# The end of a one-core transformer layer: last bank's weights gated ahead of their split, second rows' last bank in halves, squares on VectorE, epsilon as a column

## The chip, the cores and the metric

The kernel runs on one core of a Trainium2 chip. The metric is device time in microseconds (us), the median over several executions. A core has five engines, each with its own instruction queue that it works through in order: TensorE (PE; PEld is its loading of stationary weights), VectorE (DVE), ScalarE (ACT), GpSimd (POOL) and SyncE (SP, which here only issues DMAs). They wait for each other by semaphores. SBUF is the on-chip memory of 128 partitions, PSUM the banks into which TensorE adds up its products.

## The reference

One layer over 256 latent tokens of width 2048 (and 256 context tokens): a half-step feed-forward network (FFN), token mixing, a second half-step FFN, then a final RMSNorm. What the change touches is the end of the second FFN and the norm behind it. In the reference's words:

```python
def rms_norm(x, g):
    xf = x.astype(jnp.float32)
    y = xf * lax.rsqrt(jnp.mean(xf * xf, axis=-1, keepdims=True) + RMS_EPS)
    return (y * g.astype(jnp.float32)).astype(x.dtype)

def half_step_ffn(x, mod, i, g, w_up, w_down):
    h = adaln(x, g, mod, i)
    a, b = jnp.split(h @ w_up, 2, axis=-1)
    return x + 0.5 * mod[:, i + 2, None, :] * ((jax.nn.silu(a) * b) @ w_down)
...
        xl = half_step_ffn(xl, mod_l, 6, g_norm[l, 2], w_ffn2_up[l], w_ffn2_down[l])
    return rms_norm(xl, g_final)
```

So per output column there is a gate (0.5 times a modulation row) and a gain (`g_final`), and per token one factor, the reciprocal root of the mean square plus epsilon, which needs all 2048 columns of that token.

## The kernel before

The products are made close to float32 accuracy out of pairs of reduced-precision values. `split` (L120 on) makes from a 128x2048 weight tile `raw` a rounded part `hi` (a copy by ScalarE, L128) and the rest `lo` (a subtraction by VectorE, L129), in two halves of 1024 columns. `mm3` (L152) then issues three matmuls per product: stationary hi with moving hi, stationary lo with moving hi, stationary hi with moving lo. In the last part the stationary operand is 128 tokens of the hidden activations, and the moving one is up to 512 columns of weights.

The 5632 hidden units of the second FFN are taken in groups of 512. The down projection of a group has four weight tiles of 1 MB, one for each bank `cb` of 512 output columns (`CB`); each tile holds four blocks of 128 hidden units (`FB`). `down` works through two groups at a time and adds the results into `acc2`, an SBUF tile of the 256 tokens: `t = 0` is the first 128 of them (the first rows), `t = 1` the second. After the group before the last, `down` also multiplies `acc2` by the gate (`half_gated`, L1030) and has GpSimd start a DMA that adds the residual `x2d` into it (`accum`, L731).

The last group is done by `last2`. It loads its four weight tiles through SP; tiles 0 and 1 go whole into buffers of their own (`hi0`, `lo0` and so on), tiles 2 and 3 through `load_split`. Then, for t = 0 and t = 1 and within each for the four banks: `block` issues 12 matmuls into a PSUM bank, VectorE gates the result (`half_gated` into `sab`) and adds it to `acc2` (L2323), ScalarE squares the sum and adds up along the row (`sumsq`, L163), and VectorE multiplies by the gain in place (`gain`, L2291), one block later than the square that reads the same columns. `ended` closes a half of the tokens: VectorE sums the four partial sums (L2296), multiplies by 1/D and adds epsilon (L2298), GpSimd raises to the power -1/2 (L2299), then ScalarE scales banks 0 and 1 (L2308) and VectorE banks 2 and 3 (L2306; for the second rows' bank 3 gain and factor in one operation, L2304), and SP stores each bank (L2309). The first rows' `ended` is a generator whose two parts are stepped between the second rows' blocks.

The order on each engine is the program's order where an instruction is pinned (`pin`), and otherwise what a scheduler made of it; within one engine nothing overtakes. In-place work on `acc2` makes waits: the gain may only overwrite a bank when its square has been read.

Of the kernel before, what the change touches and what calls it, by code (L numbers as in the profile page):

```python
# [19 lines left out]
P = 128  # L20
# [38 lines left out]
def tile_layer(ctx: ExitStack, tc: tile.TileContext, I: dict, out: bass.AP):  # L59
# [13 lines left out]
    def bank():  # L73
        return ps["mm"].tile([P, 512], F32, tag="mm", name="mm")
# [45 lines left out]
    def split(raw, n=2048):  # L120

        half = n // 2
        parts = []
        for h in range(2):
            hi = wp.tile([P, 1024], F32R, tag="hi", name="hi", bufs=4)[:, :half]
            lo = wp.tile([P, 1024], F32R, tag="lo", name="lo", bufs=4)[:, :half]
            src = raw[:, h * half : (h + 1) * half]
            scalar[0].activation(hi, src, AF.Copy)  # L128
            vector[0].tensor_tensor(lo, src, hi.bitcast(F32), op=ALU.subtract)  # L129
            parts.append((hi, lo))  # L130

        def at(w):
            h, o = divmod(w.start, half)
            return tuple(x[:, o : o + w.stop - w.start] for x in parts[h])

        return at
# [24 lines left out]
    def sumsq(dst, x, n=512):  # L161
        junk = sm.tile([P, 512], BF16, tag="junk", name="junk", bufs=1)
        scalar[0].activation(junk[:, :n], x, AF.Square, accum_out=dst)  # L163
# [103 lines left out]
    class Beside:  # L267
# [49 lines left out]
        def steps(self):  # L317
            half = None
            while self.n < len(self.items) or self.due or self.late:
                while self.n < len(self.items):  # L320
                    h = self.items[self.n][2]
                    if h != half:
                        half = h
                        conditions({LAT: self.cB}, h, h + 1, (LAT,))
                        self.waits += WAIT
                    if self.n not in self.slots or self.done < np.interp(self.n, *zip((0, 0), *self.pace)) + self.waits:
                        break
                    self.one()
                yield
                self.done += 1  # L330
                for x in [x for x in self.due if x[0] <= self.done]:
                    self.due.remove(x)
                    self.finish(*x[1:])
                if self.late and self.late[0][0] <= self.done:
                    mod_rows_out(*self.late.pop(0)[1:])

    def pin(ins):
        tc.keep_in_program_order(ins)
# [58 lines left out]
    def drain(it):  # L397
        for _ in it:
            pass
# [62 lines left out]
    with pool(name="st", bufs=1) as st:  # L462
# [53 lines left out]
        def factor(ss4):  # L516
            s1 = sm.tile([P, 1], F32, tag="s1", name="s1")
            vector[0].tensor_reduce(s1, ss4, axis=AX.X, op=ALU.add)
            r = sm.tile([P, 16], F32, tag="rstd", name="rstd", bufs=4)[:, :1]
            vector[0].tensor_scalar(r, s1, 1.0 / D, EPS, op0=ALU.mult, op1=ALU.add)  # L520
            nc.gpsimd.tensor_tensor(r, r, mhalf[:, :1], op=ALU.pow)
            return r
# [505 lines left out]
    def half_gated(a, y, g, sign=1.0):  # L1028

        nc.vector.scalar_tensor_tensor(a, y, 0.5 * sign, g, op0=ALU.mult, op1=ALU.mult)  # L1030
# [897 lines left out]
    with f2x:  # L1928
# [4 lines left out]
        def sab_tile():  # L1933
            return f2.tile([P, CB], F32, tag="sab", name="sab")
# [262 lines left out]
                                nc.scalar.activation(sab[t], bs[t], AF.Silu)  # L2197
                    yield

        def block(b, n, wt, t, first=True, last=True):  # L2200

            tt = slice(t * P, (t + 1) * P)
            for j in range(FB):
                w = slice(j * CB, (j + 1) * CB)
                mm3(b, hids[n][0][:, j, tt], hids[n][1][:, j, tt], *wt(w), first and j == 0, last and j == FB - 1)
            return b

# [67 lines left out]
        def last2():  # L2275

            parts = []
            for cb in range(NCB):
                if cb >= 2:
                    parts.append(load_split(I["w_dn2"][LAST, cb]))  # L2280
                    continue
                raw = raw_tile()
                nc.sync.dma_start(raw, I["w_dn2"][LAST, cb])
                hi = f3.tile([P, 2048], F32R, tag=f"f{2 * cb}", name=f"hi{cb}")
                lo = f3.tile([P, 2048], F32R, tag=f"f{2 * cb + 1}", name=f"lo{cb}")
                nc.scalar.activation(hi, raw, AF.Copy)
                nc.vector.tensor_tensor(lo, raw, hi.bitcast(F32), op=ALU.subtract)
                parts.append(lambda w, hi=hi, lo=lo: (hi[:, w], lo[:, w]))
            def gain(t, cb):
                a = acc2[:, t, cb * CB : (cb + 1) * CB]  # L2290
                pin(nc.vector.tensor_tensor(a, a, late["gf"][:, cb * CB : (cb + 1) * CB], op=ALU.mult))  # L2291

            def ended(t, ss):

                s1 = sm.tile([P, 1], F32, tag="s1", name="s1")
                pin(nc.vector.tensor_reduce(s1, ss, axis=AX.X, op=ALU.add))  # L2296
                r = sm.tile([P, 16], F32, tag="rstd", name="rstd", bufs=4)[:, :1]
                pin(nc.vector.tensor_scalar(r, s1, 1.0 / D, EPS, op0=ALU.mult, op1=ALU.add))  # L2298
                nc.gpsimd.tensor_tensor(r, r, mhalf[:, :1], op=ALU.pow)  # L2299
                for cb in (0, 2, 1, 3):  # L2300
                    c = slice(cb * CB, (cb + 1) * CB)
                    a = acc2[:, t, c]
                    if t and cb == 3:
                        pin(nc.vector.scalar_tensor_tensor(a, a, r, late["gf"][:, c], op0=ALU.mult, op1=ALU.mult))  # L2304
                    elif cb >= 2:
                        pin(nc.vector.tensor_scalar(a, a, r, None, op0=ALU.mult))  # L2306
                    else:
                        nc.scalar.activation(a, a, AF.Copy, scale=r)  # L2308
                    nc.sync.dma_start(out[t * P : (t + 1) * P, c], a)  # L2309
                    if not t and not cb:  # L2310
                        yield


            sss = [sm.tile([P, 4], F32, tag="ss4", name="ss4", bufs=4) for _ in range(2)]
            first = ended(0, sss[0])
            for t in range(2):
                for cb in range(NCB):
                    c = slice(cb * CB, (cb + 1) * CB)
                    b = block(bank(), LAST, parts[cb], t)
                    a = acc2[:, t, c]  # L2320
                    y = sab_tile()
                    half_gated(y, b, late["g8"][:, c])
                    nc.vector.tensor_tensor(a, a, y, op=ALU.add)  # L2323
                    sumsq(sss[t][:, cb : cb + 1], a)
                    if cb or t:
                        gain(*divmod(4 * t + cb - 1, 4))
                    if t:
                        steps(first)
            drain(ended(1, sss[1]))

        last2()

# [94 lines left out]
```

## Time and profile before

| | |
|---|---|
| median of 3 runs | 2600.66 us (2600.51 to 2602.32) |
| the profiled execution | 2601.07 us |
| its span, first to last instruction | 2599.4 us |
| PE busy | 2572.7 us (99%) |
| DVE busy | 2189.6 us (84%) |
| ACT busy | 1429.8 us (55%) |
| POOL busy | 220.9 us (8%) |
| last matmul starts | 2588.41 us |
| last weight tile issued | 2562.79 us |
| last power on POOL starts | 2592.58 us |

Rows of an engine in order of time read: start and length in us, engine, source line, operation, what it writes and reads, form, and in brackets the idle time before it with what ended it. An `xN` at the end means N such instructions merged, their length running from the first start to the last end. Instructions of one engine overlap a little in the records: the step from one start to the next is what one costs in a full queue. Window rows give, for a stretch, the busy time of each engine, the granted clock of TensorE (1.00 is full) and the DMA traffic.

### The profile page before, as it was taken

The page shows a single profiled execution, that of the slowest core. Times are in us where ns is not written, and L with a number is a line of the kernel's source. Part 1 is how long each engine was busy: PE and PEld are TensorE (multiplying, and loading weights), DVE is VectorE, ACT ScalarE, POOL GpSimd, SP SyncE. Part 2 cuts the span into 40 slices and gives each one's busy share as a digit, 9 for nine tenths or more (in the row PEclk, how much of TensorE's full clock was granted, in tenths as well). Part 3 has the DMA queues.
Part 4 walks back from the last instruction along what each step waited for, and adds up shares of the span by engine and source line. Part 5 has one row for each costly group of instructions (what it writes and reads, how often), then busy time and mean ns, then how long its engine had stood idle before and what let it go on. Part 6 is the DMA issues. An engine that isn't in the chain of part 4 may idle for free. (4 is left out here: it accounts for less than half of the span.)

```text
span 2599.4 us, 34147 instructions
## 1 busy us (share of the span) xinstructions
PE 2572.7 (99%) x12646; PEld 2139.5 (82%) x12646; DVE 2189.6 (84%) x2884; ACT 1429.8 (55%) x1838; POOL 220.9 (8%) x271
## 2 busy tenths in 40 slices
PE   8999999999999999999999999999999999999998
PEld 5788888888888878888889889888898788888886
DVE  7788888878888788888887888798889788898887
ACT  5454444554444555444454448456486676666663
POOL 0000000100000100000110000120000000000001
PEclk9999999999999999999999999999999999999999
DMA  9889999999999989889987886775768999999985
GB/s 397 349 216 266 270 284 273 260 275 285 260 286 270 275 238 243 217 217 223 227 258 263 295 318 241 238 278 214 265 237 245 266 272 278 288 285 278 271 250 168
DMA packets 127655, 684.71 MB, mean 263 GB/s; under 512 B 14200, under 2 KB 16760, under 8 KB 64896
## 3 DMA queue, kind: packets, MB, share of 16 engines
q1 hardware_dynamic: 98112, 490.63, 50.2%
q0 software_dynamic: 29376, 191.90, 37.5%
q8 instruction: 99, 1.62, 0.2%
q14 instruction: 68, 0.56, 0.1%
HBM read 664.59 MB, written 17.89 MB: 263 GB/s over the span
## 5 line engine op out<-in xcount | busy, mean ns | idle before, releaser
L128 ACT ACTIVATE hi<-raw 128x1024 fp32r<-128x1024 f32 (+2 forms) x488 | 505.4, 1040 | 412.4 <-PE mm L152 309.3
L129 DVE TENSOR_TENSOR lo<-raw,hi 128x1024 fp32r<-128x1024 f32 (+2 forms) x476 | 568.9, 1204 | 143.6 <-ACT hi L128 121.7
L128 ACT ACTIVATE hi<-chain 128x1024 fp32r<-128x1024 f32 x352 | 371.9, 1060 | 310.5 <-PE mm L152 169.5
L129 DVE TENSOR_TENSOR lo<-chain,hi 128x1024 fp32r<-128x1024 f32 x352 | 426.6, 1221 | 109.9 <-ACT hi L128 100.7
L152 PE MATMUL mm<-hi,hhi 128*128 128x512 f32 (+3 forms) x1024 | 394.0, 385 | 0.0
L152 PE MATMUL mm<-lo,hhi 128*128 128x512 f32 (+3 forms) x1024 | 387.0, 378 | 0.0
L152 PE MATMUL mm<-hi,hlo 128*128 128x512 f32 (+3 forms) x1024 | 386.4, 377 | 0.0
L208 DVE SCALAR_TENSOR_TENSOR junk<-sraw,cBh 128x1024 fp8e5<-128x1024 f32 x192 | 234.4, 1221 | 16.2 <-DMA sraw<-in_w_mt 14.0
L152 PEld LDWEIGHTS mm<-lo,hhi 128*128 128x128 f32 x1024 | 192.4, 188 | 34.2 <-DVE lo L129 0.3
L152 PEld LDWEIGHTS mm<-hi,hlo 128*128 128x128 f32 x1024 | 192.8, 188 | 30.7
L152 PEld LDWEIGHTS mm<-hi,hhi 128*128 128x128 f32 x1024 | 192.6, 188 | 31.0
L129 DVE TENSOR_TENSOR lo<-ra,hi 128x1024 fp32r<-128x1024 f32 x104 | 126.1, 1221 | 30.9 <-ACT hi L128 27.0
L128 ACT ACTIVATE hi<-ra 128x1024 fp32r<-128x1024 f32 x104 | 109.8, 1061 | 66.1 <-PE mm L152 35.2
L152 PE MATMUL mm<-hi,hid2h 128*128 128x512 f32 x352 | 137.1, 389 | 0.0
L152 PE MATMUL mm<-lo,hid2h 128*128 128x512 f32 x352 | 137.0, 389 | 0.0
L152 PE MATMUL mm<-hi,hid2l 128*128 128x512 f32 x352 | 137.0, 389 | 0.0
L152 PE MATMUL mm<-hi,sumshl 128*128 128x512 f32 x400 | 123.2, 389 | 0.0
L731 POOL DMA_DIRECT2D chain<-in_w_up1b x60 | 53.0, 884 | 727.7 <-DVE lo L129 727.7
L208 DVE SCALAR_TENSOR_TENSOR sr<-sr,cBl 128x1024 f32<-128x1024 f32 x84 | 102.0, 1222 | 13.4 <-DMA sr<-in_w_mt 6.4
L152 PE MATMUL mm<-hi,sumshh 128*128 128x512 f32 x352 | 108.4, 389 | 0.0
L152 PE MATMUL mm<-hhi,hi 128*128 128x512 f32 (+1 forms) x288 | 101.3, 352 | 0.0
L152 PE MATMUL mm<-hhi,lo 128*128 128x512 f32 (+1 forms) x288 | 99.0, 344 | 0.0
(490 smaller groups left out, 5453.8 us busy)
## 6 DMA issues: line engine op xcount, KB each, us to landing
raw<-in_w_dn SPq DMA_DIRECT2D x70, 1024.0 KB, 10.1
chain<-in_w_up1b POOLq DMA_DIRECT2D x60, 1024.0 KB, 10.2
sraw<-in_w_mt SPq DMA_DIRECT2D x96, 512.0 KB, 8.0
sr<-in_w_mt SPq DMA_DIRECT2D x81, 512.0 KB, 5.6
raw<-in_w_up1b SPq DMA_DIRECT2D x40, 1024.0 KB, 7.7
mraw<-in_w_m SPq DMA_DIRECT2D x32, 1024.0 KB, 7.5
chain<-in_w_dn POOLq DMA_DIRECT2D x30, 1024.0 KB, 8.4
chain<-in_w_up2b POOLq DMA_DIRECT2D x28, 1024.0 KB, 12.6
```

Source lines behind the costliest of these rows:

```text
L128: scalar[0].activation(hi, src, AF.Copy)
L129: vector[0].tensor_tensor(lo, src, hi.bitcast(F32), op=ALU.subtract)
L152: tensor[0].matmul(out_ap, s, m, start=first and not n, stop=last and n == 2, skip_group_check=skip)
L208: ins = nc.vector.scalar_tensor_tensor(junk() if junk else raw, raw, 1.0, cB[s], op0=ALU.mult, op1=ALU.mult, accum_out=mT[:, i, s, kt, h : ...
L731: accum = lambda dst, src: nc.gpsimd.dma_start(dst, src, accum_op=ALU.add)
```

## The change

All of it is in `last2`, apart from a column offset `c0` in `block`.

- The last weight tile (`cb == 3`) is multiplied by the gate in place, four times 128x512 by VectorE, before `split`. The block of that bank then needs no gating: VectorE adds PSUM straight into `acc2`.
- The gain row `gf` is multiplied once by the square root of D (ScalarE, 128x2048). The factor is then the power -1/2 of (sum of squares + D times epsilon). D times epsilon stands as a fifth column beside the partial sums, filled by GpSimd (the tile of the sums is now 16 columns wide, under the name `rstd`), so the sum takes it in and the operation at L2298 goes away.
- The first rows' four banks are all scaled by ScalarE (two were VectorE's), their factor is made right after their last bank, and their scaling and storing is written between the second rows' blocks.
- The second rows' banks 0 and 1 get their gain right behind their own block, bank 2 between the halves of bank 3.
- The second rows' last bank is computed in two halves of 256 columns, in PSUM banks of their own; VectorE squares these halves and adds up along the row (`squared`), where ScalarE squared the whole bank.
- The second rows' banks are stored in the order 2, 0, 3, 1 (written before as 0, 2, 1, 3).

```diff
@@ -2197,11 +2197,11 @@
                                 nc.scalar.activation(sab[t], bs[t], AF.Silu)
                     yield
 
-        def block(b, n, wt, t, first=True, last=True):
+        def block(b, n, wt, t, first=True, last=True, c0=0):
 
             tt = slice(t * P, (t + 1) * P)
             for j in range(FB):
-                w = slice(j * CB, (j + 1) * CB)
+                w = slice(j * CB + c0, j * CB + c0 + b.shape[1])
                 mm3(b, hids[n][0][:, j, tt], hids[n][1][:, j, tt], *wt(w), first and j == 0, last and j == FB - 1)
             return b
 
@@ -2276,57 +2276,91 @@
 
             parts = []
             for cb in range(NCB):
-                if cb >= 2:
+                if cb == 2:
                     parts.append(load_split(I["w_dn2"][LAST, cb]))
                     continue
                 raw = raw_tile()
                 nc.sync.dma_start(raw, I["w_dn2"][LAST, cb])
+                if cb == 3:
+                    for j in range(FB):
+                        w = raw[:, j * CB : (j + 1) * CB]
+                        half_gated(w, w, late["g8"][:, 3 * CB :])
+                    parts.append(split(raw))
+                    continue
                 hi = f3.tile([P, 2048], F32R, tag=f"f{2 * cb}", name=f"hi{cb}")
                 lo = f3.tile([P, 2048], F32R, tag=f"f{2 * cb + 1}", name=f"lo{cb}")
                 nc.scalar.activation(hi, raw, AF.Copy)
                 nc.vector.tensor_tensor(lo, raw, hi.bitcast(F32), op=ALU.subtract)
                 parts.append(lambda w, hi=hi, lo=lo: (hi[:, w], lo[:, w]))
-            def gain(t, cb):
-                a = acc2[:, t, cb * CB : (cb + 1) * CB]
-                pin(nc.vector.tensor_tensor(a, a, late["gf"][:, cb * CB : (cb + 1) * CB], op=ALU.mult))
-
-            def ended(t, ss):
-
-                s1 = sm.tile([P, 1], F32, tag="s1", name="s1")
-                pin(nc.vector.tensor_reduce(s1, ss, axis=AX.X, op=ALU.add))
+            pin(nc.scalar.activation(late["gf"], late["gf"], AF.Copy, scale=D ** 0.5))
+            H = CB // 2
+            col = lambda t, cb: acc2[:, t, cb * CB : (cb + 1) * CB]
+            gf = lambda cb: late["gf"][:, cb * CB : (cb + 1) * CB]
+
+            def multiplied(t, cb):
+                pin(nc.vector.tensor_tensor(col(t, cb), col(t, cb), gf(cb), op=ALU.mult))
+
+            def squared(dst, x):
+                y = sab_tile()[:, :H]
+                pin(nc.vector.scalar_tensor_tensor(y, x, 1.0, x, op0=ALU.mult, op1=ALU.mult, accum_out=dst))
+
+            def factor(ss):
+                s = sm.tile([P, 1], F32, tag="s1", name="s1")
+                pin(nc.vector.tensor_reduce(s, ss, axis=AX.X, op=ALU.add))
                 r = sm.tile([P, 16], F32, tag="rstd", name="rstd", bufs=4)[:, :1]
-                pin(nc.vector.tensor_scalar(r, s1, 1.0 / D, EPS, op0=ALU.mult, op1=ALU.add))
-                nc.gpsimd.tensor_tensor(r, r, mhalf[:, :1], op=ALU.pow)
-                for cb in (0, 2, 1, 3):
-                    c = slice(cb * CB, (cb + 1) * CB)
-                    a = acc2[:, t, c]
-                    if t and cb == 3:
-                        pin(nc.vector.scalar_tensor_tensor(a, a, r, late["gf"][:, c], op0=ALU.mult, op1=ALU.mult))
-                    elif cb >= 2:
-                        pin(nc.vector.tensor_scalar(a, a, r, None, op0=ALU.mult))
-                    else:
-                        nc.scalar.activation(a, a, AF.Copy, scale=r)
-                    nc.sync.dma_start(out[t * P : (t + 1) * P, c], a)
-                    if not t and not cb:
-                        yield
-
-
-            sss = [sm.tile([P, 4], F32, tag="ss4", name="ss4", bufs=4) for _ in range(2)]
-            first = ended(0, sss[0])
-            for t in range(2):
-                for cb in range(NCB):
-                    c = slice(cb * CB, (cb + 1) * CB)
+                nc.gpsimd.tensor_tensor(r, s, mhalf[:, :1], op=ALU.pow)
+                return r
+
+            def store(t, cb):
+                nc.sync.dma_start(out[t * P : (t + 1) * P, cb * CB : (cb + 1) * CB], col(t, cb))
+
+            sss = [sm.tile([P, 16], F32, tag="rstd", name="rstd", bufs=4) for _ in range(2)]
+            for ss in sss:
+                nc.gpsimd.memset(ss[:, 4:5], D * EPS)
+
+            def finished(t, cb):
+                a = col(t, cb)
+                if cb == 3:
                     b = block(bank(), LAST, parts[cb], t)
-                    a = acc2[:, t, c]
+                    pin(nc.vector.tensor_tensor(a, a, b, op=ALU.add))
+                else:
+                    b = block(bank(), LAST, parts[cb], t)
                     y = sab_tile()
-                    half_gated(y, b, late["g8"][:, c])
-                    nc.vector.tensor_tensor(a, a, y, op=ALU.add)
-                    sumsq(sss[t][:, cb : cb + 1], a)
-                    if cb or t:
-                        gain(*divmod(4 * t + cb - 1, 4))
-                    if t:
-                        steps(first)
-            drain(ended(1, sss[1]))
+                    pin(nc.vector.scalar_tensor_tensor(y, b, 0.5, late["g8"][:, cb * CB : (cb + 1) * CB], op0=ALU.mult, op1=ALU.mult))
+                    pin(nc.vector.tensor_tensor(a, a, y, op=ALU.add))
+                sumsq(sss[t][:, cb : cb + 1], a)
+
+            for cb in range(NCB):
+                finished(0, cb)
+                if cb:
+                    multiplied(0, cb - 1)
+            r0 = factor(sss[0][:, :5])
+            multiplied(0, 3)
+
+            for cb in range(NCB - 1):
+                finished(1, cb)
+                if cb < 2:
+                    multiplied(1, cb)
+                for q in ((0,), (1,), (2, 3))[cb]:
+                    nc.scalar.activation(col(0, q), col(0, q), AF.Copy, scale=r0)
+                    store(0, q)
+            for h in range(2):
+                b = block(bank()[:, :H], LAST, parts[3], 1, c0=h * H)
+                a = col(1, 3)[:, h * H : (h + 1) * H]
+                pin(nc.vector.tensor_tensor(a, a, b, op=ALU.add))
+                squared(sss[1][:, 3 + 2 * h : 4 + 2 * h], a)
+                if not h:
+                    multiplied(1, 2)
+            r = factor(sss[1][:, :6])
+            for cb in (2, 0, 3, 1):
+                a = col(1, cb)
+                if cb == 3:
+                    pin(nc.vector.scalar_tensor_tensor(a, a, r, gf(3), op0=ALU.mult, op1=ALU.mult))
+                elif cb == 2:
+                    pin(nc.vector.tensor_scalar(a, a, r, None, op0=ALU.mult))
+                else:
+                    nc.scalar.activation(a, a, AF.Copy, scale=r)
+                store(1, cb)
 
         last2()
 
```

## The prediction

> **What bounds the kernel now.** I read the page first, then the last 32 us by stage (busy time by window), then the chain of waits there, then VectorE, ScalarE, GpSimd and TensorE in order of time. The page:
>
> ```profile
> span 2599.4 us, 34147 instructions
> PE 2572.7 (99%) x12646; PEld 2139.5 (82%) x12646; DVE 2189.6 (84%) x2884; ACT 1429.8 (55%) x1838; POOL 220.9 (8%) x271
> PEclk9999999999999999999999999999999999999999
> ```
>
> TensorE is busy for 99% of the span at full granted clock, so the body goes by the count of matmuls, which the change leaves alone; only the end is in play. The stages of the end (columns: stretch, length, busy time with instructions of PE, PEld, DVE, ACT, POOL, then clock, DMA share, GB/s):
>
> ```profile
> 2572.00:2588.80 16.80, 16.80 (x75) 13.57 (x73) 16.06 (x27) 6.96 (x16) 1.43 (x2) 1.00 0.24 57
> 2590.40:2592.00 1.60, 0.00 (x0) 0.00 (x0) 1.47 (x3) 0.60 (x2) 0.00 (x0) 1.00 0.04 14
> 2592.00:2594.00 2.00, 0.00 (x0) 0.00 (x0) 1.15 (x4) 0.96 (x4) 0.55 (x1) 0.53 0.00 0
> ```
>
> TensorE stops at 2588.8; VectorE is full (16.06 of 16.80) and runs on. So it is VectorE's queue, from the landing of the last weight tile to the last reciprocal root, that sets the end. That landing is on the chain of waits (start, length, what):
>
> ```profile
> 2562.79 8.47 DMA raw<-in_w_dn
> ```
>
> It lands at 2562.79 + 8.47 = 2571.26. VectorE after it (start, length, line, operation; L1030 and L2323 are a block's gating and adding, L2291 the gain, L2296 and L2298 the sum and epsilon):
>
> ```profile
> 2568.01 0.68 DVE L2226 TENSOR_TENSOR acc<-acc,mm 128x512 f32<-128x512 f32 x1
> 2568.72 0.69 DVE L1030 SCALAR_TENSOR_TENSOR acc<-acc,g 128x512 f32<-128x512 f32 x1
> 2572.46 1.23 DVE L129 TENSOR_TENSOR lo<-raw,hi 128x1024 fp32r<-128x1024 f32 x1 [3.05 <-ACT hi L128]
> ...
> 2574.20 1.22 DVE L129 TENSOR_TENSOR lo<-raw,hi 128x1024 fp32r<-128x1024 f32 x1
> 2575.34 0.68 DVE L1030 SCALAR_TENSOR_TENSOR acc<-acc,g 128x512 f32<-128x512 f32 x1
> 2575.94 0.68 DVE L1030 SCALAR_TENSOR_TENSOR sab<-mm,g 128x512 f32<-128x512 f32 x1
> 2576.66 0.69 DVE L2323 TENSOR_TENSOR acc<-acc,sab 128x512 f32<-128x512 f32 x1
> ...
> 2585.17 0.15 DVE L2298 TENSOR_SCALAR rstd<-s 128x1 f32<-128x1 f32 x1
> 2585.24 0.68 DVE L1030 SCALAR_TENSOR_TENSOR sab<-mm,g 128x512 f32<-128x512 f32 x1
> ...
> 2590.61 0.69 DVE L2323 TENSOR_TENSOR acc<-acc,sab 128x512 f32<-128x512 f32 x1
> ...
> 2592.15 0.16 DVE L2296 TENSOR_REDUCE s<-ss 128x1 f32<-128x4 f32 x1 [0.25 <-ACT junk L163]
> ```
>
> Starts tell the prices: a 512-wide operation takes 0.60 of VectorE when the next is independent (2575.34 to 2575.94), 0.72 when the next reads its result (2575.94 to 2576.66); a split half 1.14 (2574.20 to 2575.34). ScalarE and GpSimd:
>
> ```profile
> 2571.37 2.01 ACT L128 ACTIVATE hi<-raw 128x1024 fp32r<-128x1024 f32 x2 [4.72 <-DMA raw<-in_w_dn]
> ...
> 2586.01 1.34 ACT L2308 ACTIVATE acc<-acc,rstd 128x512 f32<-128x512 f32 x2 [0.72 <-POOL rstd L2299]
> 2587.25 0.61 ACT L163 ACTIVATE junk<-acc 128x512 bf16<-128x512 f32 x1
> ...
> 2591.39 0.63 ACT L163 ACTIVATE junk<-acc 128x512 bf16<-128x512 f32 x1 [1.21 <-DVE acc L2323]
> 2591.93 0.19 ACT L163 ACTIVATION_READ_ACCUMULATOR junk<-acc 128x1 f32 x1
> 2593.16 1.33 ACT L2308 ACTIVATE acc<-acc,rstd 128x512 f32<-128x512 f32 x2 [1.04 <-POOL rstd L2299]
> ```
>
> ```profile
> 2585.41 0.56 POOL L2299 TENSOR_TENSOR rstd<-rstd,mhalf 128x1 f32<-128x1 f32 x1 [8.11 <-DVE rstd L2298]
> 2592.58 0.55 POOL L2299 TENSOR_TENSOR rstd<-rstd,mhalf 128x1 f32<-128x1 f32 x1 [6.61 <-DVE rstd L2298]
> ```
>
> Two scalings occupy ScalarE for 1.24 (2586.01 to 2587.25), so 0.62 each. A sum of squares reaches VectorE 0.85 after the add that it follows (2590.61 + 0.69 = 2591.30 to the reduce at 2592.15). The last root ends at 2592.58 + 0.55 = 2593.13; from there 6.27 us run to the end of the span (2599.4).
>
> **The change part by part.** I follow the chain in the changed order, with these prices.
>
> *Gating ahead of the split.* Four new 128x512 products on VectorE (2.4 us) scale the raw tile in place. They need the landing, so they cannot start before 2571.3, and both the copy to hi and the subtraction wait for them. In the built order VectorE has after L2226 (2568.01): product 0, the row gating that stood at 2568.72, the second L2226, product 1, the second row gating, products 2 and 3, then the two split halves. Seven at 0.60 from 2571.35: product 1 starts at 2573.15, product 3 at 2574.95. Of the idle time that VectorE had from 2569.4 to 2572.46 only the part from 2571.35 is used, and the row gating that stood ahead of it now stands behind the wait. Halves of the split: ScalarE's first copy 2573.88 to 2574.94 is in time, VectorE's first half starts at 2575.55; the second copy, behind product 3 (2575.64), ends at about 2576.74, the second half starts at 2576.76, and the first block's gating at 2577.90. That was 2575.94: **+1.96**. The two row gatings release GpSimd's adding loads; the one for the first rows' last bank starts some 3 us later (about 2573.0) and is wanted at 2583.1:
>
> ```profile
> acc<-x2d POOLq DMA_DIRECT2D x8, 256.0 KB, 5.5
> ```
>
> (median to landing over the last 75 us), so it stays covered by some 4.5 us.
>
> *TensorE.* Its matmuls, the nearest 256-wide ones first:
>
> ```profile
> 1936.79 0.28 PE L152 MATMUL tr<-h2hi,lo 128*128 128x256 f32 x1
> 1936.91 0.28 PE L152 MATMUL tr<-h2hi,hi 128*128 128x256 f32 x1
> ...
> 2575.49 0.39 PE L152 MATMUL mm<-lo,hid2h 128*128 128x512 f32 x1
> ...
> 2588.18 0.39 PE L152 MATMUL mm<-hi,hid2l 128*128 128x512 f32 x1
> 2588.41 0.39 PE L152 MATMUL mm<-lo,hid2h 128*128 128x512 f32 x1
> ```
>
> The first rows' last bank wants its first lo half at 2575.49 (its third matmul) and gets it at 2576.8: an idle time of 1.3 us, after which TensorE runs about 1.3 late. The last block in halves is 24 matmuls 256 wide in place of 12 of 512; the narrow ones start 0.12 apart, the wide ones 0.227 on average: 24 x 0.12 = 2.88 against 12 x 0.227 = 2.72: 0.16 more. TensorE would end at about 2590.3. VectorE reads the last half at 2595.0 (below), so all this costs nothing; with that cover gone it would cost 1.5.
>
> *First rows.* From 2577.90: blocks 0 and 1 at 1.32 each, gain, block 2, gain: the last bank's add, now straight from PSUM and without its 0.72 of gating, starts at 2583.06 and ends at 2583.75. Its sum is reduced 0.85 later, at 2584.60 (before: about 2585.0; a short stall of 0.3, since one gain alone lies between). The epsilon operation is gone (0.15, and a hop); the root goes from 2584.84 to 2585.40, ScalarE scales from 2585.44. That is 0.57 earlier than 2586.01: the gating is paid back here, by two operations and by the order.
>
> *First rows scaled by ScalarE.* This takes two products of 0.4 from VectorE and puts four scalings, 4 x 0.62 = 2.48, on ScalarE. In the built order all four stand ahead of the second rows' first square: it starts at 2587.92 and delivers at 2588.65. VectorE has the gain of that same bank directly behind its add, in place, so it must wait for the square. It gets there early: gain of the first rows' bank 3 at 2584.67, gating 2585.27, add 2585.99, gain ready to go at 2586.59, and it starts at 2588.68. **A new wait of 2.1 us**, and everything of the second rows queues behind it on VectorE. Before, a gain stood one block later than its square and no wait of that kind shows.
>
> *Second rows.* Gating 2589.28, add 2590.00 to 2590.69, and the gain of bank 1 again right behind its own square: 2590.69 + 0.85 = 2591.54 instead of 2590.60, **a second wait of 0.9**. Bank 2: gating 2592.14, add 2592.86 to 2593.55.
>
> *Halves and VectorE's squares.* Operations of 256 columns are priced by a group of the same shape, and a product with an accumulated sum by the long ones:
>
> ```profile
> L1939 DVE TENSOR_TENSOR hid2l<-sab,hid2h 128x256 fp32r<-128x256 f32 x4 | 1.7, 418 | 0.0
> L208 DVE DVE_READ_ACCUMULATOR sr<-sr,cBl 128x1 f32 x84 | 6.8, 81 | 0.0
> ```
>
> First half's add 2593.46, its square 2593.90, the gain of bank 2 at 2594.40 (its square on ScalarE ends then), second add 2595.00, second square 2595.44 to 2595.86. The accumulator read has a bound of nothing (it can lie within the product's drain) and of 0.08 each; I take nothing, since both ends are small, and keep the 0.16. Reduce 2595.90, no epsilon, root 2596.14 to **2596.69**.
>
> *After the root.* The same four scalings on the same engines. The order of the stores changes, but their issue (two in 0.89 us) is already the limit from the second on: nothing, or 0.1 either way. The gain row's scaling (128x2048, as long as a weight copy of that size) costs ScalarE 1.92:
>
> ```profile
> 2594.58 0.89 SPq L2309 DMA_DIRECT2D out<-acc  x2
> ```
>
> ```profile
> 2555.05 1.92 ACT L2286 ACTIVATE hi<-raw 128x2048 fp32r<-128x2048 f32 x1 [3.46 <-DMA raw<-in_w_dn]
> ```
>
> It runs from 2576.7 to 2578.7, before the first square is due at 2579.3: nothing, 0.6 of cover. Two tiny GpSimd fills for the epsilon columns land beside the roots at 1904:
>
> ```profile
> L1911 DVE TENSOR_SCALAR rr<-ones,rstd x2: 288/288/288, 1904.7 to 1905.2; 128x128 f32<-128x128 f32 x2
> L1912 PEld LDWEIGHTS tr<-ident,rr x4: 190/190/192, 1909.2 to 1909.5; 128*128 128x128 f32 x4
> ```
>
> TensorE uses that result 4 us later, so they are covered.
>
> **Sum.** 2596.69 - 2593.13 = +3.56 us, of which about +2 is gating, +3.0 the two waits, and -1.4 the operations taken from VectorE. The profiled execution took 2601.07, 1.67 more than its span and 0.4 above the median; against the median of 2600.66 the forecast is 2600.66 + 3.56 = **2604.2**. That is 0.14%, less than the 0.2% (5.2 us) that a measurement of this kernel can tell from no change.
>
> **Rivals.** (a) *The squares do not hold the gains back* (ScalarE quicker, or VectorE later, than I have it). Without the two waits the same walk ends its root at about 2593.75: +0.6, 2601.3. For it: VectorE had no such wait before. Against: the built order and the in-place gain leave no choice. (b) *Slower beyond the bound: the first rows' late adding load.* If it takes longer than 10 us from 2573.0, the add at 2583.06 waits, and the roots, ScalarE and all of the second rows with it, one for one. At 12.6 us, what the slowest group of GpSimd's loads on the page needs at four times the size, it costs 2.5 more: 2606.7.
>
> ```profile
> chain<-in_w_up2b POOLq DMA_DIRECT2D x28, 1024.0 KB, 12.6
> ```
>
> Against: the queue is nearly empty then (57 GB/s in the stage). It decides from 11.7 us. (c) *The clock falls in TensorE's new idle time.* Windows show the granted clock still 1.00 up to 2592.0 and 0.53 after, 3.3 us behind the last matmul; 1.3 us is too short, and the split would have to come 2 us later. At half clock to the end the remaining 46 wide and 24 narrow matmuls would take 46 x 0.45 + 24 x 0.24 = 26.5 from 2576.8, the root would end near 2605, and the time be about 2612.5. The Trainium skill ("TensorE: Matmul & The Clock Gate", What's actually happening) has the clock halve after an idle window of about 3.4 us and return after as long a busy one; the trace agrees on the fall with its 3.3. By that rule a fall would add about 1.7 us to TensorE, which VectorE's lag would hide. (d) *Faster*: by more than 5.2 us would need the root at 2588, before the last matmul; no mechanism gives it.
>
> **How the numbers follow.** Forecast 0.80, (a) 0.07, (b) 0.05, (c) 0.02, and 0.06 for prices missed by some tenths at each of the dozen links, which lean to slower since each late link adds a wait. The forecast's own range is 2603.0 to 2605.4; with (a) in part, the accumulator reads, and the spread of the runs (2600.51 to 2602.32) I give 2602.5 to 2606.0. Faster 0.02, within 0.86, slower 0.12.
>
> **What would show it.** Gating right: VectorE's first block gating near 2577.9 and TensorE idle for about 1.3 near 2575.5. Waits right: the second rows' first two gains each begin after idle time that a ScalarE square ended, about 2.1 and 0.9 us. Root at 2596.7, end at 2603.0. Wrong if the gains start without idle time, if the raw tile lands elsewhere than at 2571, or if VectorE waits for TensorE in the halves.

## The result and the profile after

| | before | after |
|---|---|---|
| median of 22 runs each | 2599.89 us (2595.64 to 2604.33) | 2604.81 us (2598.84 to 2609.08) |
| ratio after / before | | 1.0017, 95% interval 1.0011 to 1.0023 |
| the profiled execution, its span | 2601.07, 2599.4 us | 2601.28, 2599.6 us |
| first use of the last weight tile | 2571.37 | 2567.50 |
| end of the second root on GpSimd | 2593.12 | 2593.40 |
| the tail, from the one to the other | 21.75 | 25.90 |

The changed kernel is slower by 0.17%, about 4.4 us of 2600 (interval 2.9 to 6.0). The medians alone differ by 4.92. The forecast had been +3.56 us. The prediction held that nothing below 5.2 us could be told from no change; with 22 runs of each kernel the interval keeps clear of 1. With more runs the kernel before has a median 0.8 lower than the three that the forecast started from.

The two profiled spans are nearly equal, and that misleads. Whole times of one kernel differ by some 10 us from run to run. The profiled execution of after lies 3.5 us below its own median (2601.28 against 2604.81), that of before 1.2 above its own (2601.07 against 2599.89). The 4.7 us between these two displacements is the 3.9 by which the last tile comes sooner in after's profile, and a little more. So profiles are compared here by the tail: from the first use of the last weight tile (after: VectorE's first gating product on it; before: ScalarE's first copy of it) to the end of the second root. It grew by 25.90 - 21.75 = 4.15 us (the rows are rounded, so a sum of two of them can differ from these ends by 0.01).

The page after, and then its windows over the end (columns as in the prediction):

```profile
span 2599.6 us, 34179 instructions
PE 2570.0 (99%) x12658; PEld 2139.7 (82%) x12658; DVE 2191.4 (84%) x2887; ACT 1433.6 (55%) x1839; POOL 221.2 (9%) x273
```

```profile
2567.50:2586.60 19.10, 18.67 (x93) 15.42 (x91) 16.29 (x25) 10.00 (x17) 2.63 (x3) 1.00 0.33 82
2586.60:2589.60 3.00, 0.00 (x1) 0.00 (x0) 2.10 (x4) 0.72 (x2) 0.00 (x0) 1.00 0.01 2
2589.60:2592.00 2.40, 0.00 (x0) 0.00 (x0) 2.32 (x6) 0.72 (x2) 0.00 (x0) 0.86 0.00 0
```

The page shows 12 more matmuls (the halves). That TensorE is 2.7 us less busy all the same belongs to the part ahead of the last tile, where this execution was 3.9 ahead. The windows show the end: TensorE misses 0.43 us of its 19.1 and is done at 2586.6, its clock full to the last matmul, while VectorE is 16.29 busy in 19.1 and has nearly 7 us of work and waits left. VectorE after the first use, in order of time (L1030 on `raw` gates the tile, L2329 and L2330 gate and add a block, L2325 and L2350 add bank 3 straight, L2301 is the gain, L2305 the halves' squares):

```profile
2567.50 0.69 DVE L1030 SCALAR_TENSOR_TENSOR raw<-raw,g 128x512 f32<-128x512 f32 x1 [0.96 <-DMA raw<-in_w_dn]
...
2574.15 0.68 DVE L2329 SCALAR_TENSOR_TENSOR sab<-mm,g 128x512 f32<-128x512 f32 x1
...
2579.34 0.68 DVE L2325 TENSOR_TENSOR acc<-acc,mm 128x512 f32<-128x512 f32 x1
2579.93 0.69 DVE L2301 TENSOR_TENSOR acc<-acc,gf 128x512 f32<-128x512 f32 x1
2580.87 0.16 DVE L2309 TENSOR_REDUCE s<-rstd 128x1 f32<-128x5 f32 x1 [0.25 <-ACT junk L163]
2580.95 0.68 DVE L2301 TENSOR_TENSOR acc<-acc,gf 128x512 f32<-128x512 f32 x1
...
2582.26 0.69 DVE L2330 TENSOR_TENSOR acc<-acc,sab 128x512 f32<-128x512 f32 x1
2585.29 0.69 DVE L2301 TENSOR_TENSOR acc<-acc,gf 128x512 f32<-128x512 f32 x1 [2.33 <-ACT junk L163]
...
2588.16 0.69 DVE L2301 TENSOR_TENSOR acc<-acc,gf 128x512 f32<-128x512 f32 x1 [0.85 <-ACT junk L163]
...
2592.08 0.42 DVE L2305 SCALAR_TENSOR_TENSOR sab<-acc 128x256 f32<-128x256 f32 x1
2592.43 0.08 DVE L2305 DVE_READ_ACCUMULATOR sab<-acc 128x1 f32 x1
2592.55 0.16 DVE L2309 TENSOR_REDUCE s<-rstd 128x1 f32<-128x6 f32 x1
```

Both new waits are there, 2.33 and 0.85, each ended by a square of ScalarE (`junk`), and each in front of a gain. What ScalarE does in the first of them, what GpSimd does ahead of that, and the one idle time of TensorE:

```profile
2582.08 2.56 ACT L2345 ACTIVATE acc<-acc,rstd 128x512 f32<-128x512 f32 x4 [1.25 <-POOL rstd L2311]
2584.55 0.61 ACT L163 ACTIVATE junk<-acc 128x512 bf16<-128x512 f32 x1
2585.07 0.19 ACT L163 ACTIVATION_READ_ACCUMULATOR junk<-acc 128x1 f32 x1
```

```profile
2569.20 0.88 POOL L731 DMA_DIRECT2D acc<-x2d  x1 [9.21 <-DVE acc L1030]
...
2581.18 0.87 POOL L2311 TENSOR_TENSOR rstd<-s,mhalf 128x1 f32<-128x1 f32 x1 [9.30 <-DVE s L2309]
2592.86 0.55 POOL L2311 TENSOR_TENSOR rstd<-s,mhalf 128x1 f32<-128x1 f32 x1 [10.80 <-DVE s L2309]
```

```profile
2572.99 0.50 PE L152 MATMUL mm<-lo,hid2h 128*128 128x512 f32 x1 [0.43 <-DVE lo L129]
```

The second rows' first bank is summed at 2582.26 + 0.69 = 2582.95, but its square stands on ScalarE behind four scalings and starts at 2584.55. The chain of waits (start, length, what) goes through exactly this:

```profile
2581.18 0.88 POOL rstd L2311
2582.08 0.92 ACT acc L2345 x2
...
2583.33 1.32 ACT acc L2345 x2
2584.65 0.62 ACT junk L163 x2
2585.29 0.04 DVE acc L2301
...
2587.41 0.73 ACT junk L163 x2
2588.16 0.04 DVE acc L2301
```

### The profile page after: what moved, and what is told of

Read it like the earlier page. It is cut to its first block, busy times and chain, and to the rows that moved or that the text cites. A ratio compares the mean times of both kernels' runs of the same rounds, so it can differ in the third digit from the quotient of the medians.

```text
span 2599.6 us, 34179 instructions
## 1 busy us (share of the span) xinstructions
PE 2570.0 (99%) x12658; PEld 2139.7 (82%) x12658; DVE 2191.4 (84%) x2887; ACT 1433.6 (55%) x1839; POOL 221.2 (9%) x273
## 5 line engine op out<-in xcount | busy, mean ns | idle before, releaser
L152 PE MATMUL mm<-lo,hid2h 128*128 128x512 f32 (+1 forms) x356 | 137.8, 387 | 0.4 <-DVE lo L129 0.4
L152 PE MATMUL mm<-hi,hid2h 128*128 128x512 f32 (+1 forms) x356 | 137.8, 387 | 0.0
L152 PE MATMUL mm<-hi,hid2l 128*128 128x512 f32 (+1 forms) x356 | 137.7, 387 | 0.0
```

The lines of the kernel that those rows point to most:

```text
L152: tensor[0].matmul(out_ap, s, m, start=first and not n, stop=last and n == 2, skip_group_check=skip)
```

## The experiments

The expectations name the theories by letters: W is the prediction's account, that the two waits in front of the in-place gains cost most of the time; B, that the time lies in the body and not in the tail; G, that the gating of the tile costs it; H is on what the halves are worth; P, that the first root is slowed by the product that VectorE runs beside it. All tails are measured as above. Each kernel's tail comes from one profile; the ratios come from the runs.

| kernel | first use | tail | last matmul's start to end of root | first root took | ratio to before, 95% |
|---|---|---|---|---|---|
| before | 2571.37 | 21.75 | 4.71 | 0.56 | |
| after | 2567.50 | 25.90 | 7.08 | 0.87 | 1.0017 (1.0011 to 1.0023) |
| gains a block later | 2567.64 | 23.50 | 4.70 | 0.87 | 1.0006 (0.9997 to 1.0014) |
| squares between the scalings | 2566.05 | 24.43 | 5.61 | 0.87 | 0.9999 (0.9990 to 1.0008) |
| both | 2568.78 | 22.40 | 3.58 | 0.87 | 1.0003 (0.9995 to 1.0012) |
| no gating of the tile | 2568.05 | 25.34 | 7.99 | 0.87 | 1.0016 (1.0008 to 1.0025) |
| gating alone, on before | 2567.07 | 22.08 | 3.14 | 0.56 | 1.0007 (0.9998 to 1.0015) |
| another product beside the root | 2567.66 | 24.98 | 6.18 | 0.56 | 1.0011 (1.0002 to 1.0019) |
| second rows' last bank whole | 2567.28 | 25.14 | 6.59 | 0.87 | 1.0011 (1.0002 to 1.0021) |
| third tile gated, done last | 2568.84 | 21.18 | 2.56 | 0.56 | 0.9992 (0.9984 to 1.0001) |

The two lengths need not agree: after's end is 4.15 longer than before's by the tail, but 2.37 longer from the last matmul (7.08 - 4.71), since the landing of the tile and the stream of matmuls do not keep the same distance from profile to profile. The ratio of after (2.9 to 6.0 us) goes with the tail.

**Gains a block later.** The second rows' gains go back to where before had them, one block behind their squares.

```diff
                 finished(1, cb)
-                if cb < 2:
-                    multiplied(1, cb)
+                if cb:
+                    multiplied(1, cb - 1)
```

> The changed kernel, with the second rows' gains of banks 0 and 1 one block later than their squares, as the kernel before had them; nothing else. The yardstick is the tail: from the first use of the last weight tile to the end of the second root. It is 21.8 us in the profile of before (2571.37 to 2593.13) and 25.9 in that of the changed kernel (2567.50 to 2593.41). Theory W (VectorE's two waits for ScalarE's squares, 2.3 and 0.85 us, carry the loss): the first wait shrinks to under 1 us and the second goes, tail 23.6, time 1.0007 of before. Rival G (the gating ahead of the split, which makes VectorE's first block and TensorE late, carries it): the waits only hide that, tail still 25.5 to 25.9. Rival B (the tail is not where the time goes, the body is): the tail may move, the ratio stays at 1.0017.

VectorE at the first of these gains, and at the next:

```profile
2585.43 0.69 DVE L2301 TENSOR_TENSOR acc<-acc,gf 128x512 f32<-128x512 f32 x1 [1.01 <-ACT junk L163]
...
2587.36 0.68 DVE L2301 TENSOR_TENSOR acc<-acc,gf 128x512 f32<-128x512 f32 x1
```

The second wait is gone, the first is down from 2.33 to 1.01: one block (gating and add, 1.32) stands in it. The tail loses 2.40, more than half of what the change had added, with all arithmetic kept.

**Squares between the scalings.** ScalarE's order alone: square, scaling, square, scaling, square, two scalings, instead of four scalings ahead of the first square.

```diff
-                sumsq(sss[t][:, cb : cb + 1], a)
+                junk = sm.tile([P, 512], BF16, tag="junk", name="junk", bufs=1)
+                pin(nc.scalar.activation(junk, a, AF.Square, accum_out=sss[t][:, cb : cb + 1]))
...
-                    nc.scalar.activation(col(0, q), col(0, q), AF.Copy, scale=r0)
+                    pin(nc.scalar.activation(col(0, q), col(0, q), AF.Copy, scale=r0))
```

> The changed kernel, with ScalarE held to the written order: the square of second rows' bank 0 ahead of the first rows' scalings, and these spread behind the squares of banks 0, 1 and 2. The gains stay where the change put them. W: each of the two gains still waits 0.85 to 0.95 us for the square directly ahead of it, but the first no longer for four scalings of 2.5 us: tail 24.5, time 1.0010 of before. G: 25.5 to 25.9. B: ratio 1.0017.

```profile
2582.38 0.69 DVE L2301 TENSOR_TENSOR acc<-acc,gf 128x512 f32<-128x512 f32 x1 [0.87 <-ACT junk L2332]
...
2585.25 0.69 DVE L2301 TENSOR_TENSOR acc<-acc,gf 128x512 f32<-128x512 f32 x1 [0.85 <-ACT junk L2332]
```

Now both waits have the same length, that of a square that starts at once: 0.87 and 0.85. The tail loses 1.47. So the first wait of 2.33 had two parts: 1.46 for the four scalings in front of the square, 0.87 for the square itself. Here tail and ratio do not quite agree: a tail of 2.68 more than before's would be 1.0010, and the interval of the ratio ends at 1.0008.

**Both.** The two edits above together.

> Both of the foregoing: gains one block later, and ScalarE in the written order. W: no wait of VectorE for ScalarE is left in the second rows' blocks, tail 22.8, 1.0 more than before; time 1.0004 of before. G: 25 or more, with VectorE waiting for TensorE instead. B: ratio 1.0017.

```profile
2585.48 0.69 DVE L2301 TENSOR_TENSOR acc<-acc,gf 128x512 f32<-128x512 f32 x1
...
2587.41 0.68 DVE L2301 TENSOR_TENSOR acc<-acc,gf 128x512 f32<-128x512 f32 x1
2588.01 0.41 DVE L2351 TENSOR_TENSOR acc<-acc,mm 128x256 f32<-128x256 f32 x1
```

No gain waits any more. The tail is 22.40: of the 4.15 that the change added, 3.50 are gone, and 0.65 are left for everything else in it. G falls as the account of the loss, for the tile is still gated ahead of its split here. The ratio of 1.0003 can no longer be told from 1. So B falls too: with the tail the time went as well.

**No gating of the tile.** From after: the last tile goes through `load_split` like the third, and its block is gated behind the matmuls, each half too.

```diff
-                if cb == 2:
+                if cb >= 2:
                     parts.append(load_split(I["w_dn2"][LAST, cb]))
...
-                if cb == 3:
-                    b = block(bank(), LAST, parts[cb], t)
-                    pin(nc.vector.tensor_tensor(a, a, b, op=ALU.add))
...
-                pin(nc.vector.tensor_tensor(a, a, b, op=ALU.add))
+                y = sab_tile()[:, :H]
+                pin(nc.vector.scalar_tensor_tensor(y, b, 0.5, late["g8"][:, 3 * CB + h * H : 3 * CB + (h + 1) * H], op0=ALU.mult, op1=ALU.mult))
+                pin(nc.vector.tensor_tensor(a, a, y, op=ALU.add))
```

> The changed kernel without the gating ahead of the split: the last tile is split as it lands, and its block, or each half of it, is gated behind the matmuls as the other banks are. W: VectorE's first block starts 2.0 us sooner, but the first rows' last bank costs 0.7 more and the two halves 0.45 each at the end, and both waits stay: tail 25.5, time 1.0015 of before. G: the tail falls by the whole 2.0 or more, to 23.9 or less, time 1.0008. B: ratio 1.0017.

ScalarE's first copy of the tile, then VectorE's first block gating and the gains that wait, then the first root (three views of this kernel):

```profile
2568.05 2.01 ACT L128 ACTIVATE hi<-raw 128x1024 fp32r<-128x1024 f32 x2 [2.17 <-DMA raw<-in_w_dn]
```

```profile
2572.62 0.68 DVE L2319 SCALAR_TENSOR_TENSOR sab<-mm,g 128x512 f32<-128x512 f32 x1
...
2584.49 0.69 DVE L2295 TENSOR_TENSOR acc<-acc,gf 128x512 f32<-128x512 f32 x1 [2.34 <-ACT junk L163]
...
2587.35 0.69 DVE L2295 TENSOR_TENSOR acc<-acc,gf 128x512 f32<-128x512 f32 x1 [0.85 <-ACT junk L163]
```

```profile
2580.38 0.87 POOL L2305 TENSOR_TENSOR rstd<-s,mhalf 128x1 f32<-128x1 f32 x1 [6.39 <-DVE s L2303]
```

The first block gating comes 2572.62 - 2568.05 = 4.57 after the first use, as in before; in after it is 2574.15 - 2567.50 = 6.65. So the gating ahead of the split delays VectorE by 2.08. The first root ends 2580.38 + 0.87 - 2568.05 = 13.20 after the first use, in after 2581.18 + 0.87 - 2567.50 = 14.55: of the 2.08 the missing gating of the first rows' last bank has paid back 0.73. The two gatings of the halves pay back more than half of the rest, and the whole tail is only 0.56 shorter. The waits are the same to 0.01, and the ratio is that of after: the gating is not the main cost. By the tail it costs 0.56 of the 4.15, which is too little for these ratios to show.

**Gating alone, on before.** The tile is gated ahead of its split and bank 3 added straight, nothing else.

```diff
-                if cb >= 2:
+                if cb == 2:
...
+                if cb == 3:
+                    for j in range(FB):
+                        w = raw[:, j * CB : (j + 1) * CB]
+                        half_gated(w, w, late["g8"][:, 3 * CB :])
+                    parts.append(split(raw))
+                    continue
...
-                    y = sab_tile()
-                    half_gated(y, b, late["g8"][:, c])
+                    y = b
+                    if cb < 3:
+                        y = sab_tile()
+                        half_gated(y, b, late["g8"][:, c])
```

> The kernel before with one part of the change alone: the last weight tile multiplied by the gate ahead of its split, and its two blocks added without gating. The tail (first use of the last tile to the end of the second root) is 21.8 us in the kernel before. W: the first block starts 2.0 later, and two gatings of 0.7 fall away: tail 22.3, time 1.0002 of before, no wait of VectorE for ScalarE in the second rows. G (the gating carries the loss): tail 24 or more, time 1.0012 or more.

The two ends of this kernel's tail, VectorE's first product on the tile and the second root:

```profile
2567.07 0.69 DVE L1030 SCALAR_TENSOR_TENSOR raw<-raw,g 128x512 f32<-128x512 f32 x1 [0.44 <-DMA raw<-in_w_dn]
```

```profile
2588.60 0.55 POOL L2305 TENSOR_TENSOR rstd<-rstd,mhalf 128x1 f32<-128x1 f32 x1 [5.87 <-DVE rstd L2304]
```

The tail is 22.08, 0.33 more than before, and no gain in it waits. Alone the gating is nearly neutral. The interval of the ratio holds both 1 and the 1.0001 that the tail gives; the medians alone (2602.33 against 2600.17) would have said something else. The interval reaches to 1.0015 and so does not exclude the 1.0012 of G by itself; the tail does, for G asked for 24 or more.

**Another product beside the root.** From after: the gain of the first rows' bank 3 stands behind the second rows' first block, so that VectorE gates a block out of PSUM while GpSimd takes the root. The edit has a side effect: only three scalings stand ahead of the first square.

```diff
             r0 = factor(sss[0][:, :5])
-            multiplied(0, 3)
...
                 finished(1, cb)
+                if not cb:
+                    multiplied(0, 3)
```

> The changed kernel with one VectorE instruction moved: the gain of the first rows' bank 3, which runs beside the first root on GpSimd, comes after the next block's gating and adding. The first root took 0.87 us in the changed kernel and its offspring, 0.56 in the kernel before. Theory P (GpSimd waits while VectorE's product of two SBUF tensors runs beside it): with a product beside it that reads PSUM and one SBUF tensor, as before, the root takes 0.56 again. Rival: 0.87 as ever, and the cause lies in the root's input. Beside that, ScalarE gets three scalings in place of four ahead of the square of second rows' bank 0: by W the first wait loses 0.6 of scaling and what the root gains, and part of it is filled by the moved gain: tail 25.0.

VectorE, and then GpSimd, of this kernel:

```profile
2581.10 0.68 DVE L2329 SCALAR_TENSOR_TENSOR sab<-mm,g 128x512 f32<-128x512 f32 x1
...
2584.53 0.69 DVE L2301 TENSOR_TENSOR acc<-acc,gf 128x512 f32<-128x512 f32 x1 [1.42 <-ACT junk L163]
```

```profile
2581.34 0.56 POOL L2311 TENSOR_TENSOR rstd<-s,mhalf 128x1 f32<-128x1 f32 x1 [9.30 <-DVE s L2309]
```

The root is back at 0.56: P stands. The tail is 0.92 shorter. That fits 0.31 for the root and about 0.6 for the one scaling less ahead of the square; the first wait fell by 0.91 (2.33 to 1.42).

**Second rows' last bank whole.** From after: no halves, the square by ScalarE, the gain of bank 2 behind it.

```diff
-            for cb in range(NCB - 1):
+            for cb in range(NCB):
                 finished(1, cb)
...
-                for q in ((0,), (1,), (2, 3))[cb]:
+                for q in ((0,), (1,), (2, 3), ())[cb]:
...
-            for h in range(2):
...
-            r = factor(sss[1][:, :6])
+            multiplied(1, 2)
+            r = factor(sss[1][:, :5])
```

> The changed kernel with the second rows' last bank whole again: 12 matmuls of 512, one add, and its square by ScalarE; the gain of bank 2 behind the add. W: VectorE is far behind TensorE there, so the halves hide nothing and cost VectorE two more operations and two squares; without them the root comes 0.9 sooner: tail 25.0, time 1.0014 of before. Rival H (the halves shorten the end, as they would with TensorE late): tail 26.4 or more.

```profile
2589.89 0.68 DVE L2325 TENSOR_TENSOR acc<-acc,mm 128x512 f32<-128x512 f32 x1
2590.82 0.69 DVE L2301 TENSOR_TENSOR acc<-acc,gf 128x512 f32<-128x512 f32 x1 [0.25 <-ACT junk L163]
2591.57 0.16 DVE L2309 TENSOR_REDUCE s<-rstd 128x1 f32<-128x5 f32 x1
```

From the start of the last bank's add to the reduce it takes 2591.57 - 2589.89 = 1.68, in halves 2592.55 - 2590.10 = 2.45 (the first half's add in after starts at 2590.10). The tail is 0.76 shorter. Halves are meant to let VectorE work on one half while the matmuls of the next are still running. In after TensorE was done at 2586.60, before VectorE came to the first half at all, and the halves only put two squares on VectorE that ScalarE had time for. H falls.

**Third tile gated, done last.** From "both": the third weight tile is gated ahead of its split instead of the fourth, and its bank is the second rows' last, in halves; the first rows' bank 3 gets its gain behind the second rows' first block.

```diff
-                if cb == 2:
+                if cb == 3:
                     parts.append(load_split(I["w_dn2"][LAST, cb]))
...
-            multiplied(0, 3)
-
-            for cb in range(NCB - 1):
+            for cb in (0, 1, 3):
                 finished(1, cb)
-                if cb:
-                    multiplied(1, cb - 1)
+                multiplied(*((1, cb // 2) if cb else (0, 3)))
...
-                b = block(bank()[:, :H], LAST, parts[3], 1, c0=h * H)
+                b = block(bank()[:, :H], LAST, parts[2], 1, c0=h * H)
```

> A version meant to beat both: the changed kernel with both waits taken away (gains one block later, ScalarE in the written order, the first rows' bank 3 gained after the next block), and the third weight tile gated ahead of its split in place of the fourth, since VectorE is idle between its landing and that of the fourth; the second rows work on bank 2 last, in the halves, so neither half needs gating. W: VectorE is no longer behind TensorE at the end: from the start of the last matmul to the end of the second root about 2.0 us (before 4.7, changed kernel 7.1), tail 19.4, time 0.9991 of before. Rival: the gating of the third tile delays the split of it or of the fourth, TensorE idles, and the tail is 21.5 or more.

VectorE's longest wait ahead of the last root, and its end; then the chain of waits over the same stretch:

```profile
2584.91 0.69 DVE L2329 SCALAR_TENSOR_TENSOR sab<-mm,g 128x512 f32<-128x512 f32 x1 [0.39 <-PE mm L152]
...
2588.25 0.41 DVE L2349 TENSOR_TENSOR acc<-acc,mm 128x256 f32<-128x256 f32 x1
...
2589.17 0.16 DVE L2309 TENSOR_REDUCE s<-rstd 128x1 f32<-128x6 f32 x1
```

```profile
2559.94 24.95 PE mm L152 x110
```

TensorE runs without a gap from 2559.94 to 2584.89, and VectorE waits for it, not the other way round. From the start of the last matmul to the end of the root it takes 2.56, in before 4.71, so by this measure 2.15 us of the end are gone. The tail says less. Its two ends, ScalarE's first copy of the fourth tile and the second root:

```profile
2568.84 1.06 ACT L128 ACTIVATE hi<-raw 128x1024 fp32r<-128x1024 f32 x1
```

```profile
2589.47 0.55 POOL L2311 TENSOR_TENSOR rstd<-s,mhalf 128x1 f32<-128x1 f32 x1 [8.09 <-DVE s L2309]
```

That is 21.18, only 0.57 less than before, where the expectation had 19.4: here it missed, though TensorE does not idle as the rival had it. Here TensorE and not the last tile's landing sets the end, so the tail is the weaker measure of the two. The ratio is 0.9992, which would be 2.1 us, but its interval (0.9984 to 1.0001) holds either gain and touches 1: that this kernel beats before is not shown.

## Why the prediction was right

The time came out at 2604.81 where 2604.2 was forecast. The step of +3.56 measured +4.15 in the tail and +4.4 (2.9 to 6.0) by the ratio. That the absolute time was met to 0.6 is in part luck: the median that the forecast started from was 0.8 high, and against the medians' difference of 4.92 its step is 1.4 short. Point by point, as distances from the first use of the tile (the prediction's own places less 2571.35, after's less 2567.50):

| step | forecast | measured |
|---|---|---|
| first block gating | 6.55 | 6.65 |
| first rows' sum reduced | 13.25 | 13.37 |
| ScalarE's first scaling | 14.09 | 14.58 |
| second rows' first gain (wait) | 17.33 (2.1) | 17.79 (2.33) |
| second gain (wait) | 20.19 (0.9) | 20.66 (0.85) |
| bank 2's gain, between the halves | 23.05 | 23.53 |
| last reduce | 24.55 | 25.05 |
| root's end | 25.34 | 25.90 |

- **The waits**: right, in place, releaser and nearly in size. The two together were 3.18 against 3.0, and taking both away took 3.50 off the tail.
- **The mis-sized term: the first root.** The prediction took 0.56 for it, as in before; it took 0.87, since the gain of the first rows' bank 3 now runs beside it. The prediction's own walk has that gain and the root at the same time (2584.67 and 2584.84), but it gave the meeting no price. Of the 0.56 by which the tail missed, 0.31 came in here, between the reduce and the first scaling (the two rows with 0.12 and 0.49 between forecast and measured). The scalings, the square and the first wait all slid by it. From there on the walk keeps its distance.
- **Gating ahead of the split**: +1.96 forecast, 2.08 measured against the same kernel without it. Most of it is paid back behind, as the prediction's walk had it: all but 0.56 in after, all but 0.33 alone on before.
- **TensorE's idle time**: 0.43, not 1.3. The prediction set the tile's landing against matmuls of before's profile; in after's profile the tile came sooner against them. It was hidden in either case: VectorE read the last half long after TensorE's end.
- **Adding load** (rival b): issued at 2569.20, wanted at 2579.34, and the add there starts without idle time. The rival fell.
- **Clock** (rival c): 1.00 to the last matmul, 0.86 in the window from 2589.60 to 2592.00, so it fell no sooner than 3.0 behind TensorE's end at 2586.60, and the 0.43 of idle time did not move it. The rival fell.
- **Accumulator reads**: recorded at 0.08, inside the product's end (2592.08 + 0.42 = 2592.50, the read ends at 2592.51, the reduce starts at 2592.55). Nothing, as taken.
- **Rival (a)**, no waits, put the root at +0.6: the kernel with both edits has +0.65. The walk was right for a kernel that this change had not been.
- **A sign that was wrong**: the prediction called itself wrong "if the raw tile lands elsewhere than at 2571", and gave 2577.9, 2596.7 and 2603.0 as places. All of them lay some 3 to 4 us earlier (2574.15, 2593.40, and 2599.6 for the end of the span). Places on the clock of one execution are no test where whole runs differ by 10 us; distances from the landing are, and these held.

Left open: the ratio after "squares between the scalings", lower than its tail by somewhat more than its interval; and what the last kernel gains in time, 2 us as from its last matmul, 0.6 as by its tail, or nothing.

## What to carry to other kernels

An in-place operation right behind the square that reads the same columns waits for that square's whole way through another engine (0.85 us here), and for everything the other engine has queued ahead of it (1.46 more): keep one block of other work between the two, and look at the order on the engine that is *not* the bottleneck. When an engine is the bound at the end, count what stands in its queue and what it waits for; work taken from it (here 1.4 us by the prediction's count) is soon lost to one wait. Compare ends by distances from a common event, not by the spans of two executions, and choose an event that the end hangs on.

## What the runs showed of the hardware

At the end of these kernels GpSimd's root of 128x1 takes 0.55 or 0.56 alone or beside a VectorE product that reads PSUM and one SBUF tensor, and 0.87 when VectorE multiplies two SBUF tensors (2580.95 to 2581.63 in after, the root from 2581.18). VectorE's product takes its usual 0.68 in both cases. The Trainium skill ("SBUF — State Buffer", SBUF: two separate sides) says that the two engines share a port pair which is locked for a whole instruction, and that a VectorE operation with two SBUF inputs takes it against a GpSimd operation that reads SBUF. The trace agrees on which product slows the root. By that lock the root could not have read before 2581.63, 0.45 after its recorded start; the record shows 0.31 more, so part of a root's 0.56 seems to need no port, an estimate from one shape.

The profile of before shows the wait more plainly further up, where GpSimd scales a 128x4 tile. That takes 0.19 with no such product beside it (at 1729.34), but here:

```profile
1740.62 1.23 DVE L129 TENSOR_TENSOR lo<-raw,hi 128x1024 fp32r<-128x1024 f32 x1 [0.23 <-ACT hi L128]
...
1740.74 1.15 POOL L157 TENSOR_SCALAR rstd<-mss 128x4 f32<-128x4 f32 x1
```

It ends at 1741.89, 0.04 behind VectorE's product (1741.85). Who starts first matters: near the start of the same profile, VectorE's squaring product of an SBUF tile with itself makes a root that starts 0.17 behind it take 0.93 (15.32 against 15.15), and a root that starts 0.10 ahead of the next such product takes 0.59 (17.10 against 17.20). The product keeps its 0.68 there, so that VectorE is held in its turn, as a lock in both directions would have it, does not show.
